# Attention maps of both token tiles in one stage, with a PSUM ring in the planner

## The chip, the core and the metric

One core of a Trainium2 chip runs the whole program. The metric is the device time of one execution in microseconds (us). Names used below: PE is TensorE (matmuls and transposes), DVE is VectorE, ACT is ScalarE, POOL is GpSimd, SP issues the weight transfers. PSUM is the memory that PE writes its results to; a PSUM tile here is one bank of 128 x 512 fp32.

## The reference

Two layers; each has a mixer part, a convolutional feed-forward part and a gated embedding. The change lies in the mixer part:

```python
proj = u @ w_in      # -> qa ka va | qi ki wi | qb kb vb | gate_a gate_b
# mixer A: 8 heads, one shared key/value head, 64 best keys of each query by the indexer
logit = einsum('bthd,btkd->bthk', qa, k_sel) * scale_a
o_a = einsum('bthk,btkd->bthd', softmax(where(valid, logit, -inf)), v_sel)
# mixer B: 4 heads with two softmax maps each, over all earlier keys
a1 = softmax(where(causal, s1, -inf)); a2 = softmax(where(causal, s2, -inf))
o_b = einsum('bhts,bshe->bthe', a1 - lam * a2, vb)
o_b = rms_norm(o_b, g_subln) * (1 - lam_init)
mix = sigmoid(gate_a) * (o_a @ w_branch_a) + sigmoid(gate_b) * (o_b @ w_branch_b)
h = h + mix @ w_out
```

There are 256 tokens and 1024 channels. Mixer A is computed densely: the selection is an additive mask of 0 or -1e30.

## The kernel before, in words

The 256 tokens are two tiles of 128 (`i` = 0 and 1); tile `i` sees 128 * (i + 1) keys. All weights stream from HBM as 128 chunks of 128 x 1024 a layer. Each chunk is split into a high part `wh` (ACT, line 164) and a rest `wl` (DVE, line 179), and each product is three matmuls: high by `wh`, high by `wl`, rest by `wh` (lines 352 to 354, function `gemm_a`). One chunk feeds 12 such matmuls. These streams are the main work of PE: the projections and gates read `u`, the two branch products read `o`, the output product reads `m`. The branch products come in a fixed order: 48 matmuls for mixer B, a point at which the program insists that mixer A is finished, then 48 for mixer A.

The mixers' own work is small and is slipped between these streams by a planner (`class Side`). It holds Python generators ("threads"), each a chain of steps that issue instructions and yield how long the step should keep PE, DVE and ACT busy. After every 12 stream matmuls `tick` runs each thread that the planner's model thinks ready, by priority. The model only decides where in the program an instruction stands; on the chip every engine takes its instructions in that order and waits by semaphores. `side.until(flag)` ticks with no stream between, until a step is done: once for mixer B ("ob") at the end of the gates, and once for mixer A before its branch product.

A map step (`maps`, lines 585 to 608) makes the scores of 4 maps of one token tile and one half of the heads (`hq`). PE first adds the mask (line 596: identity by mask, bf16, on the whole 128-row array), then the products (line 628 for B, 633 for A), which contract over 64 rows and so use half of the array, two at a time. DVE takes maxima (`mx`, `nb`), ACT takes 4 exponentials with sums (line 605). Each map step takes 2 of the 4 PSUM tiles named `tp`. Then the thread normalises on DVE (line 645 or 689), transposes on PE (line 620), copies on ACT (`pt`, line 621), and multiplies by the values on PE (line 656 for B, 699 for A). Mixer B also needs the norm of its result: squares on ACT (`osq`, line 661), `oss` on DVE, a power on POOL (line 262), `ob` on DVE (line 669); `ob` is transposed at the end (line 315, names `ident,ob`). Eight map steps in a layer: 2 mixers x 2 halves of the heads x 2 token tiles.

Of the kernel before, what the change touches and what calls it, by code (L numbers as in the profile page):

```python
# [9 lines left out]
F32 = mybir.dt.float32  # L10
# [7 lines left out]
P = 128  # L18
# [27 lines left out]
ORDER_A = [(0, 1), (1, 1), (0, 0), (1, 0)]  # L46
ORDER_B = [(0, 1), (0, 0), (1, 1), (1, 0)]
# [12 lines left out]

class Side:
# [6 lines left out]
    def __init__(self):  # L68
        self.threads = []
        self.pe = self.dve = self.act = 0.0  # L70

    def spawn(self, gen, prio=1):
        self.threads.append([prio, gen, 0.0])
        self.threads.sort(key=lambda t: t[0])
# [8 lines left out]
    def tick(self):  # L83
        start = self.pe
        for t in list(self.threads):
            if t[2] > self.pe or self.dve > self.pe + LIMIT_US or self.pe > start + SIDE_US:
                continue
            try:
                pe, dve, act = next(t[1])
            except StopIteration:  # L90
                self.threads.remove(t)
                continue
            self.pe += pe
# [16 lines left out]
def decoder_kernel(ctx: ExitStack, tc: tile.TileContext, x, pT, ws, fc, tb, gf, rope, out):  # L110
# [170 lines left out]
    def b4(name, dt=F32):  # L281
        return blk.tile([P, 4, L], dt, tag="blk", name=name)

    class HL:
# [18 lines left out]
    def split_T2(srcs, hf, k0, scale, x, between=None):  # L303


        hi, lo = x.two(4 * hf + k0)
        n = 1 if callable(scale) else 2
        pts = []
        for a in range(0, 2, n):
            pt = ps_tp.tile([P, 2, L], F32, name="tp")[:, :n, :]  # L310
# [16 lines left out]
    def split_T_side(srcs, hf, scale, x, flag):  # L327
        for k0 in (0, 2):
            split_T2(srcs, hf, k0, scale, x)
            yield 0.45, 0.8, 0.3  # L330
        flags.add(flag)
# [86 lines left out]
    def transposed(srcs, nb, dst):  # L418

        for b0 in range(0, nb, 2):  # L420
            n = min(2, nb - b0)
            pt = ps_tp.tile([P, 2, L], F32, name="tp")
# [19 lines left out]
    for l in range(DEPTH):  # L442
# [44 lines left out]
        def index_side(pi):  # L487
# [18 lines left out]
            pt = ps_tp.tile([P, 2, L], F32, name="tp")  # L506
# [9 lines left out]
            for i in range(2):  # L516
                S = P * (i + 1)
                rel = b4("rel")[:, :, :S]
                ps = [ps_tp.tile([P, 2, L], F32, name="tp") for _ in range(2)]
# [42 lines left out]
        def heads_side(pr, nm, is_q):  # L562

            rows, rq = [], []
            for i in range(2):
# [13 lines left out]
                yield 0.0, (2.8 if nm == "kb" else 2.2), 0.0  # L579
            rqs[nm] = rq  # L580
            qT[nm] = b4("qT")
# [4 lines left out]
        def maps(qn, product, i, hq, mk):  # L586
# [3 lines left out]
            mx, nb, sums = (sm.tile([P, 2, 2], F32, name=nm, bufs=4) for nm in ("mx", "nb", "sums"))  # L590
# [6 lines left out]
            for m in range(2):  # L597
                for r in range(2):
                    product(pss[r][:, m, :S], 2 * hq + m, r, slice(i * P, (i + 1) * P), S)
            for r in range(2):  # L600
                nc.vector.reduce_max(mx[:, r, :], pss[r][:, :, :S], axis=AX.X)
            nc.vector.scalar_tensor_tensor(nb, mx, -1.0, rq, op0=ALU.mult, op1=ALU.mult)
            for r in range(2):
                for m in range(2):
                    nc.scalar.activation(pe[:, 2 * m + r, :], pss[r][:, m, :S], AF.Exp,  # L605
                                         bias=nb[:, r, m:m + 1], scale=rq[:, r, m:m + 1],
                                         accum_out=sums[:, r, m:m + 1])
            return pe, sums

        def ptrans(src, nh, i):  # L610
# [4 lines left out]
            for a in range(0, n, 4):  # L615
                w = min(4, n - a)
                pt = ps_tp.tile([P, 4, P], F32, name="tp")
# [17 lines left out]
        def mixer_b(hq, i):  # L635
            while not {"qb", "kb"} <= flags:
                yield NONE
            pe, sums = maps("qb", product_b, i, hq, cmb)
            yield 0.9 + 0.9 * i, 0.8 + 0.6 * i, MA + MB * i
# [12 lines left out]
            po = ps_tp.tile([P, 4, P], F32, name="tp")[:, 0:2, :]  # L652
# [28 lines left out]
        def mixer_a(hq, i):  # L681
            while not {"qa", "mask"} <= flags:
                yield NONE
            pe, sums = maps("qa", product_a, i, hq, mask[i])
            yield 0.9 + 0.9 * i, 0.8 + 0.6 * i, MA + MB * i
# [5 lines left out]
            yield 0.0, 0.9 + 0.3 * i, 0.0  # L691
            pt = ptrans(pe, 4, i)
            yield 0.5 + 0.5 * i, 0.0, 0.5 + 0.5 * i
            nb = i + 1
            ptv = pt[:, :4 * nb, :].rearrange("p (m r s) t -> p m r s t", r=2, s=nb)
            po = ps_tp.tile([P, 2, L], F32, name="tp")[:, 0, :].rearrange("p (m t) -> p m t", t=P)
# [11 lines left out]
        def o_side():  # L708
            while not {("b", hq, i) for hq, i in ORDER_B} <= flags:
                yield NONE  # L710
            for k0 in (0, 2):
                split_T2([ob[:, 0, :], ob[:, 1, :]], 1, k0, gsub, o_parts())
                yield 0.45, 0.8, 0.3
            flags.add("ob")
# [6 lines left out]
        for hq, i in ORDER_B:  # L721
            side.spawn(mixer_b(hq, i), 1)
# [4 lines left out]
        for hq, i in ORDER_A:  # L727
            side.spawn(mixer_a(hq, i), 1)
# [19 lines left out]
        side.until(lambda: {("a", hq, i) for hq, i in ORDER_A} <= flags)  # L748
# [31 lines left out]
        def ffn_T(i, hf):  # L780
            for k in (0, 2):
                pt = ps_tp.tile([P, 4, P], F32, name="tp")[:, 0:2, :]
# [45 lines left out]
        def products(c):  # L828


            if c - C_UP >= 2:
                made[c] = chunk(l, c)
                acc = ps_tp.tile([P, 2, L], F32, name="tp")
                part_products(c, acc, range(KD))
                return acc
            if c == C_UP:
# [3 lines left out]
                accs = [ps_tp.tile([P, 2, L], F32, name="tp") for _ in cs]  # L840
# [226 lines left out]
```

## Time and profile before

| | |
|---|---|
| median of 3 runs | 789.13 us (789.01 to 789.47) |
| profiled execution, its own time | 788.99 us |
| its span, first to last instruction | 787.2 us |
| PE busy / chain that ended last, PE share | 778.2 us (99%) / 91% |
| DVE, ACT, POOL busy | 588.8, 501.3, 162.0 us |
| granted clock of TensorE | 1.00 of full speed |
| map steps of the two layers | near 65 to 126 us and 450 to 511 us |

The page gives busy time, the chain of work that ended last and the costliest groups of instructions. The timeline gives instructions in order of time; neighbours alike are merged, so the time from one row's start to the next row's start is what a step really takes on its engine, and the duration of a single matmul, which overlaps the next, is not.

### The profile page before, as it was taken

Reading aid. Unit: us, or ns where it says so; the run is one execution under the profiler, and the core shown is the slowest. Engines: PE = TensorE matmul, PEld = TensorE weight load, DVE = VectorE, ACT = ScalarE, POOL = GpSimd, SP = SyncE. Lnnn points to the kernel's source line nnn. Section 1 sums busy time; section 2 is a strip of 40 time slices with the busy share of each in tenths; the row PEclk is TensorE's granted clock in tenths of the full one; section 3 lists DMA queues with packets and bytes.
Section 4 is the critical chain, followed back from the end, with each engine's and each line's share of the span. In section 5 each row is a group of like instructions: output and inputs, shape, how many; then the busy total and the mean of one; then the engine's idle time right before and its main releaser. Section 6 shows DMA issues by size and latency. Waiting matters only on the chain.

```text
span 787.2 us, 11678 instructions
## 1 busy us (share of the span) xinstructions
PE 778.2 (99%) x4025; PEld 646.3 (82%) x4025; DVE 588.8 (75%) x1128; ACT 501.3 (64%) x886; POOL 162.0 (21%) x162
## 2 busy tenths in 40 slices
PE   8999999999999999999999999999999999999997
PEld 6877886788888888888888778778888888888886
DVE  5987997675887778854687889768668878795643
ACT  6766757455877777553576486565468777773541
POOL 0240300000344442000123213000104444400000
PEclk9999999999999999999999999999999999999999
DMA  8654353462665656646465344445636656558521
GB/s 325 213 167 155 114 198 124 152 227 94 219 206 183 197 194 210 230 157 228 134 195 177 126 142 165 148 131 193 205 121 207 204 177 204 178 181 289 183 85 54
DMA packets 40188, 139.51 MB, mean 177 GB/s; under 512 B 4544, under 2 KB 5696, under 8 KB 40128
## 3 DMA queue, kind: packets, MB, share of 16 engines
q1 hardware_dynamic: 39264, 136.91, 52.3%
q10 hardware_dynamic: 864, 1.84, 0.7%
q8 instruction: 32, 0.52, 0.3%
q14 instruction: 28, 0.23, 0.1%
HBM read 137.69 MB, written 1.05 MB: 176 GB/s over the span
## 4 chain that ended last, share of the span: by engine, by line
PE 91%; DVE 3%; ACT 3%; POOL 1%; issue 1%; DMA 1%; SPq 0%; DVEq 0%; ACTq 0%
PE tp L824 21%; PE acc L352 12%; PE acc L354 12%; PE acc L353 12%; PE tp L826 11%; PE acc L926 5%; PE acc L925 5%; PE acc L927 5%; ACT pe L605 2%; PE tp L315 2%; DVE wl L179 1%; PE tp L620 1%; PE tp L699 1%; PE tp L656 1%; PE tp L633 1%
## 5 line engine op out<-in xcount | busy, mean ns | idle before, releaser
L164 ACT ACTIVATE wh<-raw 128x1024 fp32r<-128x1024 f32 x254 | 264.1, 1058 | 37.3 <-PE acc L927 18.0
L179 DVE TENSOR_TENSOR wl<-raw,wh 128x1024 fp32r<-128x1024 f32 x178 | 213.7, 1220 | 26.5 <-ACT wh L164 26.3
L824 PE MATMUL tp<-u,wh 128*128 128x512 f32 x704 | 177.1, 392 | 0.0
L824 PEld LDWEIGHTS tp<-u,wh 128*128 128x128 f32 x704 | 126.3, 189 | 22.3
L352 PE MATMUL acc<-wh,u 128*128 128x512 f32 (+1 forms) x336 | 133.7, 398 | 0.0
L353 PE MATMUL acc<-wl,u 128*128 128x512 f32 (+1 forms) x336 | 130.5, 388 | 0.0
L354 PE MATMUL acc<-wh,u 128*128 128x512 f32 (+1 forms) x336 | 130.5, 388 | 0.0
L176 POOL TENSOR_TENSOR wl<-raw,wh 128x512 fp32r<-128x512 f32 x76 | 98.4, 1295 | 142.9 <-ACT wh L164 60.9
L826 PEld LDWEIGHTS tp<-u,wl 128*128 128x128 f32 x704 | 96.6, 190 | 7.2
L826 PE MATMUL tp<-u,wl 128*128 128x256 f32 x704 | 98.8, 282 | 0.0
L858 DVE SCALAR_TENSOR_TENSOR cv<-tp,fc,cv 128x255 f32<-128x255 f32 (+1 forms) x176 | 84.1, 478 | 3.1
L352 PEld LDWEIGHTS acc<-wh,u 128*128 128x128 f32 x336 | 63.1, 188 | 13.2 <-issue 0.7
L354 PEld LDWEIGHTS acc<-wh,u 128*128 128x128 f32 x336 | 63.1, 188 | 12.9
L353 PEld LDWEIGHTS acc<-wl,u 128*128 128x128 f32 x336 | 63.2, 188 | 11.6 <-DVE wl L179 0.2
L853 DVE TENSOR_TENSOR tp<-tp,cl 128x256 f32<-128x256 f32 x88 | 38.0, 432 | 45.9 <-ACT cl L851 45.4
L925 PE MATMUL acc<-wh,g 128*128 128x512 f32 x176 | 68.9, 391 | 0.0
L927 PE MATMUL acc<-wh,g 128*128 128x512 f32 x176 | 68.5, 389 | 0.0
L926 PE MATMUL acc<-wl,g 128*128 128x512 f32 x176 | 68.5, 389 | 0.0
L854 ACT ACTIVATE cv<-tp,fc 128x256 f32<-128x256 f32 x88 | 49.6, 564 | 25.8 <-DVE tp L853 25.3
L276 POOL TENSOR_SCALAR sst<-ss 128x2 f32<-128x2 f32 (+1 forms) x8 | 5.0, 628 | 258.7 <-ACT junk L268 258.5
L175 DVE TENSOR_TENSOR wl<-raw,wh 128x514 fp32r<-128x514 f32 x76 | 53.6, 705 | 0.0
L851 ACT ACTIVATE cl<-tp 128x256 f32<-128x256 f32 x88 | 33.5, 381 | 28.9 <-PE tp L826 28.7
(180 smaller groups left out, 1038.9 us busy)
## 6 DMA issues: line engine op xcount, KB each, us to landing
raw<-ws SPq DMA_DIRECT2D x254, 512.0 KB, 3.5
raw<-ws SPq DMA_DIRECT2D x4, 256.0 KB, 5.0
gb<-gf ACTq DMA_DIRECT2D x2, 512.0 KB, 4.6
out<-h SPq DMA_DIRECT2D x3, 256.0 KB, 2.0
h<-x SPq DMA_DIRECT2D x2, 256.0 KB, 4.3
h<-x SPq DMA_DIRECT2D x1, 512.0 KB, 6.4
px<-pT ACTq DMA_DIRECT2D x2, 256.0 KB, 2.8
tbl<-tb SPq DMA_DIRECT2D x1, 256.0 KB, 7.3
```

What stands on the lines that cost most here:

```text
L164: nc.scalar.activation(wh, raw, AF.Copy)
L176: nc.gpsimd.tensor_tensor(wl[:, b], raw[:, b], wh[:, b].bitcast(F32), op=ALU.subtract)
L179: nc.vector.tensor_sub(wl, raw, wh.bitcast(F32))
L352: nc.tensor.matmul(o, a, wh, start=q == 0, stop=False)
L353: nc.tensor.matmul(o, a, wl, start=False, stop=False)
L354: nc.tensor.matmul(o, b, wh, start=False, stop=q == nk - 1)
L824: nc.tensor.matmul(acc, wh[:, k, :], u.pair(k), start=k == 0, stop=False)
L826: nc.tensor.matmul(acc[:, 0, :], wl[:, k, :], u.hi(k), start=False, stop=k == KD - 1)
L858: nc.vector.scalar_tensor_tensor(c[:, sh:], pu[:, :L - sh], w[:, 2 - sh:3 - sh], c[:, sh:], op0=ALU.mult, op1=ALU.add)
L925: nc.tensor.matmul(acc[i], a, wh, start=k == 0, stop=False)
L926: nc.tensor.matmul(acc[i], a, wl, start=False, stop=False)
L927: nc.tensor.matmul(acc[i], b, wh, start=False, stop=k == NF - 1)
```

## The change

Both token tiles of one half of the heads now form one map step. All four mask products stand first, then all eight half-array products; the step takes all four PSUM tiles at once. The exponentials of both tiles follow, and each tile's remaining work becomes a thread of its own. The hand-written orders of the steps are gone. The planner gets a ring that models when the four PSUM tiles come free: a thread announces with `Room(n)` how many it needs, and isn't run before the model has them free. The planned cost of one step of `kb` rises from 2.8 to 3.4.

```diff
-ORDER_A = [(0, 1), (1, 1), (0, 0), (1, 0)]
-ORDER_B = [(0, 1), (0, 0), (1, 1), (1, 0)]
+EXP_US = (1.75, 2.2)
+BANK_US = 0.9
...
+    def room(self, n):
+        return all(self.free[(self.taken + j) % 4] <= self.pe for j in range(n))
...
+            if not self.room(t[3]):
+                continue
+            taken, t[3] = self.taken, 0
             try:
-                pe, dve, act = next(t[1])
+                got = next(t[1])
+                while isinstance(got, Room):
+                    t[3] = got.n
+                    got = next(t[1]) if self.room(got.n) else NONE
...
+            until = self.pe + BANK_US
+            if exp:
+                self.exp = until = max(self.exp, self.pe + LAG_US + dve) + exp[0]
+            for j in range(taken, self.taken):
+                self.free[j % 4] = until
...
-        def maps(qn, product, i, hq, mk):
+        def scores(qn, product, i, hq, mk):
...
-            pss = [ps_tp.tile([P, 2, L], F32, name="tp") for _ in range(2)]
+            pss = [tp([P, 2, L]) for _ in range(2)]
             mk2 = mk.unsqueeze(1).broadcast_to([P, 2, n])
             for r in range(2):
                 nc.tensor.matmul(pss[r][:, :, S - n:S], identb, mk2, start=True, stop=False, skip_group_check=True)
-            for m in range(2):
+            def products():
+                for m in range(2):
+                    for r in range(2):
+                        product(pss[r][:, m, :S], 2 * hq + m, r, slice(i * P, (i + 1) * P), S)
+            def exps():
...
+            return products, exps
+
+        def maps(ready, qn, product, hq, mk, rest, prio):
+            while not ready():
+                yield NONE
+            yield Room(4)
+            todo = [scores(qn, product, i, hq, mk(i)) for i in (1, 0)]
+            for products, _ in todo:
+                products()
+            got = [exps() for _, exps in todo]
+            yield 2.0, 2.2, 2 * MA + MB, sum(EXP_US)
+            for i, g in zip((1, 0), got):
+                side.spawn(rest(hq, i, *g), prio)
...
-        def mixer_a(hq, i):
-            while not {"qa", "mask"} <= flags:
-                yield NONE
-            pe, sums = maps("qa", product_a, i, hq, mask[i])
-            yield 0.9 + 0.9 * i, 0.8 + 0.6 * i, MA + MB * i
+        def mixer_a(hq, i, pe, sums):
...
+            yield Room(i + 1)
             pt = ptrans(pe, 4, i)
             yield 0.5 + 0.5 * i, 0.0, 0.5 + 0.5 * i
+            yield Room(1)
...
-        for hq, i in ORDER_B:
-            side.spawn(mixer_b(hq, i), 1)
+        for hq in range(2):
+            side.spawn(maps(lambda: {"qb", "kb"} <= flags, "qb", product_b, hq, lambda i: cmb, mixer_b, 1), 1)
...
-        for hq, i in ORDER_A:
-            side.spawn(mixer_a(hq, i), 1)
+        for hq in range(2):
+            side.spawn(maps(lambda: {"qa", "mask"} <= flags, "qa", product_a, hq, lambda i: mask[i], mixer_a, 1), 1)
```

Three places show how the order of instructions moves. The first is PE, first layer, first map steps of mixer B (`cmb` is the causal mask, `qT` the transposed queries and keys). Before:

```order
L596 LDWEIGHTS identb
L596 MATMUL tp<-cmb,identb 128x2x128
L596 LDWEIGHTS identb
L596 MATMUL tp<-cmb,identb 128x2x128
L628 MATMUL tp<-qT 128x256 x4
L596 LDWEIGHTS identb
L596 MATMUL tp<-cmb,identb 128x2x128
L596 LDWEIGHTS identb
L596 MATMUL tp<-cmb,identb 128x2x128
L628 MATMUL tp<-qT 128x128 x4
```

And PE at the same place of the program after the change:

```order
L631 LDWEIGHTS identb
L631 MATMUL tp<-cmb,identb 128x2x128
L631 LDWEIGHTS identb
L631 MATMUL tp<-cmb,identb 128x2x128
L631 LDWEIGHTS identb
L631 MATMUL tp<-cmb,identb 128x2x128
L631 LDWEIGHTS identb
L631 MATMUL tp<-cmb,identb 128x2x128
L681 MATMUL tp<-qT 128x256 x4
L681 MATMUL tp<-qT 128x128 x4
```

The two half-array runs have become one. The second place is PE in the second layer, from the end of the gates into the branch products. Before, the last steps of mixer A stand between stream matmuls of the branch product, 12 apart (`va` are the values, `o` the branch input):

```order
L354 MATMUL acc<-wh,o 128x512
L699 MATMUL tp<-pt,va 64x256 x4
L620 MATMUL tp<-ident,pe 128x128 x4
L352 MATMUL acc<-wh,o 128x512
L353 MATMUL acc<-wl,o 128x512
L354 MATMUL acc<-wh,o 128x512
L352 MATMUL acc<-wh,o 128x512
```

After the change, PE at the end of the second layer's gates (`prv` are mixer B's values, `ob` its result):

```order
L385 MATMUL acc<-wh,u 128x512
L707 MATMUL tp<-prv,pt 128x128 x6
L673 MATMUL tp<-ident,pe 128x128 x24
L748 MATMUL tp<-pt,va 64x256 x6
L345 MATMUL tp<-ident,ob 128x128 x4
L748 MATMUL tp<-pt,va 64x256 x4
L345 MATMUL tp<-ident,ob 128x128 x4
L748 MATMUL tp<-pt,va 64x256 x2
L383 MATMUL acc<-wh,o 128x512
L384 MATMUL acc<-wl,o 128x512
```

Half of mixer B's value products, all transposes of mixer A and all its value products now stand in one run with no stream matmul between. (In the first layer the run is `ident,pe` x12, `pt,va` x6, `ident,pe` x12, `pt,va` x6, between the two branch products.) The third place is ACT at that end of the second layer, after the change, from the exponentials of mixer A's second half on:

```order
L644 ACTIVATE pe,sums<-tp,nb,rq 128x256 x4
L644 ACTIVATE pe,sums<-tp,nb,rq 128x128 x4
L189 ACTIVATE wh<-raw 128x1024 x2
L787 ACTIVATE tg<-acc,rsh 128x512 x2
L189 ACTIVATE wh<-raw 128x1024
L712 ACTIVATE osq,oss<-tp 128x128 x4
L674 ACTIVATE pt<-tp 128x512 x6
L752 ACTIVATE o<-tp 128x2x128 x2
```

The copies `pt` that the value products need stand behind all of these; before, mixer B had been finished earlier, and one or two `pt` copies at a time stood between single `wh` rows.

## Rows read from the trace of the kernel before

**Rows 1.** Page, part 1: busy us (share of the span) and instructions

```profile
PE 778.2 (99%) x4025; PEld 646.3 (82%) x4025; DVE 588.8 (75%) x1128; ACT 501.3 (64%) x886; POOL 162.0 (21%) x162
```

**Rows 2.** Timeline of PE, first map steps: start us, us, engine, line, tiles, count

```profile
64.87 0.39 PE L596 MATMUL tp<-cmb,identb 128*128 128x256 bf16 x2
65.19 1.13 PE L628 MATMUL tp<-qT 64*128 64x256 f32 x8
66.26 0.39 PE L596 MATMUL tp<-cmb,identb 128*128 128x256 bf16 x2
66.58 0.72 PE L628 MATMUL tp<-qT 64*128 64x128 f32 x8
67.22 0.50 PE L352 MATMUL acc<-wh,u 128*128 128x512 f32 x1
```

**Rows 3.** Timeline of PE, second map steps of mixer B and the next stream

```profile
70.12 0.60 PE L596 MATMUL tp<-cmb,identb 128*128 128x256 bf16 x2
...
73.05 0.50 PE L352 MATMUL acc<-wh,u 128*128 128x512 f32 x1
...
84.07 1.14 PE L620 MATMUL tp<-ident,pe 128*128 128x128 f32 x8
```

**Rows 4.** Waits: engine, line, waited for: us in total, times, longest

```profile
PE tp L596 <- ACT pe L605: 0.9, 3, 0.5
```

**Rows 5.** Timeline of PE, first map step of mixer A

```profile
117.48 0.60 PE L596 MATMUL tp<-mk,identb 128*128 128x512 bf16 x2
118.02 1.14 PE L633 MATMUL tp<-kT,qT 64*128 64x256 f32 x8
```

**Rows 6.** Timeline of PE, value products and transposes of mixer A

```profile
132.85 1.08 PE L699 MATMUL tp<-pt,va 128*64 128x256 f32 x8
133.86 1.09 PE L620 MATMUL tp<-ident,pe 128*128 128x128 f32 x8
134.71 0.47 PE L352 MATMUL acc<-wh,o 128*128 128x512 f32 x1
```

**Rows 7.** Timeline of ACT, mixer A of the first layer

```profile
120.77 0.56 ACT L605 ACTIVATE pe<-tp,nb,rq 128x256 f32<-128x256 f32 x1 [5.86 <-PE tp L633]
...
126.06 0.49 ACT L605 ACTIVATE pe<-tp,nb,rq 128x128 f32<-128x128 f32 x1
...
129.54 1.13 ACT L164 ACTIVATE wh<-raw 128x1024 fp32r<-128x1024 f32 x1
130.49 1.34 ACT L737 ACTIVATE tg<-acc,rsh 128x512 f32<-128x512 f32 x2
131.62 1.17 ACT L621 ACTIVATE pt<-tp 128x512 f32<-128x512 f32 x2
```

**Rows 8.** Timeline of DVE, mixer A of the first layer

```profile
122.19 1.22 DVE L179 TENSOR_TENSOR wl<-raw,wh 128x1024 fp32r<-128x1024 f32 x1
...
128.26 0.17 DVE L687 RECIPROCAL rcp<-sums 128x4 f32<-128x4 f32 x1
...
129.52 0.17 DVE L687 RECIPROCAL rcp<-sums 128x4 f32<-128x4 f32 x1
...
130.52 0.17 DVE L687 RECIPROCAL rcp<-sums 128x4 f32<-128x4 f32 x1
```

**Rows 9.** Timeline of ACT, squares of mixer B in the second layer

```profile
488.59 0.27 ACT L661 ACTIVATE osq<-tp 128x128 f32<-128x128 f32 x1
...
489.09 1.07 ACT L164 ACTIVATE wh<-raw 128x1024 fp32r<-128x1024 f32 x1
```

**Rows 10.** Timeline of POOL, the power for mixer B's norm

```profile
489.76 0.19 POOL L261 TENSOR_SCALAR pw<-oss 128x2 f32<-128x2 f32 x1 [5.09 <-DVE oss L664]
490.03 0.69 POOL L262 TENSOR_TENSOR ff<-pw,mhalf 128x2 f32<-128x2 f32 x1
```

**Rows 11.** Windows at the end: length, PE, PEld, DVE, ACT, POOL busy, PEclk, DMA

```profile
782.00:783.00 1.00, 0.82 (x7) 0.61 (x6) 0.89 (x3) 0.15 (x1) 0.00 (x0) 1.00 0.03 10
786.00:787.00 1.00, 0.00 (x0) 0.00 (x0) 0.00 (x0) 0.00 (x0) 0.00 (x0) 0.91 0.00 0
```

More of the change, by code (lines that the diff above doesn't have):

```diff
@@ L69, in __init__ @@
         self.threads = []
-        self.pe = self.dve = self.act = 0.0
+        self.pe = self.dve = self.act = self.exp = 0.0
+        self.free, self.taken = [0.0] * 4, 0
+    def room(self, n):
+        return all(self.free[(self.taken + j) % 4] <= self.pe for j in range(n))
     def spawn(self, gen, prio=1):
-        self.threads.append([prio, gen, 0.0])
+        self.threads.append([prio, gen, 0.0, 0])
         self.threads.sort(key=lambda t: t[0])
@@ L92, in tick @@
                 continue
+            pe, dve, act, *exp = got
+            if got is not NONE:
+                t[3] = 0
             self.pe += pe
             end = self.pe
+            until = self.pe + BANK_US
[3 more added lines that the diff above has]
+                self.free[j % 4] = until
             if dve:
@@ L282, in b4, with tp @@
         return blk.tile([P, 4, L], dt, tag="blk", name=name)
+    def tp(shape):
+        side.free[side.taken % 4] = side.pe + BANK_US
+        side.taken += 1
+        return ps_tp.tile(shape, F32, name="tp")
     class HL:
@@ L328, in split_T_side @@
         for k0 in (0, 2):
+            yield Room(2 if callable(scale) else 1)
             split_T2(srcs, hf, k0, scale, x)
@@ L421, in transposed @@
             n = min(2, nb - b0)
-            pt = ps_tp.tile([P, 2, L], F32, name="tp")
+            pt = tp([P, 2, L])
             for j in range(n):
@@ L505, in index_side @@
                 yield 0.0, 2.8, 0.0
-            pt = ps_tp.tile([P, 2, L], F32, name="tp")
+            yield Room(2)
+            pt = tp([P, 2, L])
             for j in range(2):
@@ L517, in index_side @@
                 S = P * (i + 1)
+                yield Room(2)
                 rel = b4("rel")[:, :, :S]
-                ps = [ps_tp.tile([P, 2, L], F32, name="tp") for _ in range(2)]
+                ps = [tp([P, 2, L]) for _ in range(2)]
                 for b in range(2):
@@ L596, in maps @@
                 nc.tensor.matmul(pss[r][:, :, S - n:S], identb, mk2, start=True, stop=False, skip_group_check=True)
-            for m in range(2):
-                for r in range(2):
[L599 to L608, printed above, removed]
+            def products():
[3 more added lines that the diff above has]
+            def exps():
+                for r in range(2):
+                    nc.vector.reduce_max(mx[:, r, :], pss[r][:, :, :S], axis=AX.X)
+                nc.vector.scalar_tensor_tensor(nb, mx, -1.0, rq, op0=ALU.mult, op1=ALU.mult)
+                for r in range(2):
+                    for m in range(2):
+                        nc.scalar.activation(pe[:, 2 * m + r, :], pss[r][:, m, :S], AF.Exp,
+                                             bias=nb[:, r, m:m + 1], scale=rq[:, r, m:m + 1],
+                                             accum_out=sums[:, r, m:m + 1])
+                return pe, sums
+            return products, exps
[10 more added lines that the diff above has]
+                side.spawn(rest(hq, i, *g), prio)
         def ptrans(src, nh, i):
@@ L633, in product_a, with mixer_b @@
             nc.tensor.matmul(o_, qT["qa"][rs_, b, ts], kT[rs_, :S], start=False, stop=True, skip_group_check=True)
-        def mixer_b(hq, i):
-            while not {"qb", "kb"} <= flags:
-                yield NONE
-            pe, sums = maps("qb", product_b, i, hq, cmb)
-            yield 0.9 + 0.9 * i, 0.8 + 0.6 * i, MA + MB * i
+        def mixer_b(hq, i, pe, sums):
             rcp = sm.tile([P, 2, 2], F32, name="rcp", bufs=4)
@@ L708, in o_side @@
         def o_side():
-            while not {("b", hq, i) for hq, i in ORDER_B} <= flags:
+            while not {("b", hq, i) for hq in range(2) for i in range(2)} <= flags:
                 yield NONE
             for k0 in (0, 2):
+                yield Room(1)
                 split_T2([ob[:, 0, :], ob[:, 1, :]], 1, k0, gsub, o_parts())
@@ L747, in decoder_kernel @@
             gemm_a(o["x"], range(4, 8), stream(l, C_BR + 2 * hf), 512, ev_b)
-        side.until(lambda: {("a", hq, i) for hq, i in ORDER_A} <= flags)
+        side.until(lambda: {("a", hq, i) for hq in range(2) for i in range(2)} <= flags)
         px = sm.tile([P, 2, L], F32, name="px", **T2)
@@ L839, in products @@
                     made[c_] = chunk(l, c_)
-                accs = [ps_tp.tile([P, 2, L], F32, name="tp") for _ in cs]
+                accs = [tp([P, 2, L]) for _ in cs]
                 for ks in (range(KD // 2), range(KD // 2, KD)):
```

24 lines of the change are left out of this document (14 added, 10 removed).

## Prediction

> **What bounds the kernel now.** I read the page first, then PE's timeline around the map steps, then ACT's and DVE's timelines at the same places. The page has PE busy for 99% of the span [rows 1], so time is won only where PE spends time on something else than its matmul columns, and lost wherever PE must stand still. The reader is to see three such places. A half-array run costs more than its columns [rows 2]; the second half of the heads waits for PSUM banks that the exponentials still read [rows 3, 4]; and a stream restarts slowly after each interruption [rows 2, 3]. Everything else on ACT, DVE and POOL is hidden as long as stream matmuls stand between a step and the next one that needs it. That last point is what the change touches most.
>
> **Gain 1: fewer turns between whole and half array.** Eight half-array products on 256 columns take 65.19 to 66.26 = 1.07 us, on 128 columns 66.58 to 67.22 = 0.64 [rows 2]. The difference of 0.43 is the price of 128 columns for all eight, so 1.07 contains 0.86 of columns and 0.21 of fixed cost for entering and leaving the half array. Two mask products of 256 columns take 0.32 (64.87 to 65.19), two of 512 columns 0.54 (117.48 to 118.02) [rows 2, 5]: 0.22 of columns and 0.10 fixed. The pair of steps took 64.87 to 67.22 = 2.35; the merged step has each fixed cost once: 0.10 + 0.44 + 0.21 + 0.86 + 0.43 = 2.04. So 0.31 saved per merged pair, and 4 pairs in each of 2 layers: 2.5 us. The lower bound is 0 (if the fixed cost belongs to each change of length and not to the array), the upper 0.31; I take the upper, since mask and product runs of both lengths give the same fixed part.
>
> **Gain 2: waits for banks.** The second pair of mixer B takes 70.12 to 73.05 = 2.93 against 2.35 for the first, with the same instructions: 0.58 of waiting [rows 2, 3]. The second layer has the same, and mixer A once waits 0.5; PE's own part of it is listed as 0.9 in 3 waits [rows 4]. That is 0.9 to 1.7, and I take 1.7. It goes away because the order now puts 36 or more stream matmuls between the halves of mixer B, 8.1 us at 0.226 each (the 36 more matmuls between 73.05 and 84.07 than between 67.22 and 70.12 took 8.1 us more [rows 2, 3]), and 36 (24 of `o` and 12 of `u` in the first layer) between those of mixer A. All exponentials of a merged step are over about 7.5 us after its start (below), so the banks are free. Without that cover the wait would come back, at about 0.6 each.
>
> **Gain 3: fewer restarts.** Twelve stream matmuls between two map steps take 67.22 to 70.12 = 2.90, where 12 x 0.226 is 2.71: 0.19 for one restart after the half array [rows 2, 3]. Counted in the order of instructions from the first map step to the point where the branch products run without a break, the runs of stream matmuls go from 28 to 17 in both layers together. Most of those that go stood behind transposes, whose restart I did not price and take as less; with 0.12 as a middle the 11 are worth 1.3 us, between 0.5 and 2.1.
>
> The gains sum to 2.5 + 1.7 + 1.3 = 5.5 us.
>
> **Loss: two runs with nothing between.** At the end of mixer A in the first layer, and of both mixers in the second, the program insists that the mixers be finished, and the steps now stand in one run on PE (the second place of the order). I add up each engine's queue there, from the start of mixer A's second map step as time 0. Prices, start to start: an exponential of 256 columns 0.54, of 128 columns 0.435 (120.77 to 126.06 holds eight of the first kind and one `wh`; 126.06 to 129.54 eight of the second); `wh` 0.95; `tg` 0.57; a `pt` copy 0.5, with 0.62 until its data is there [rows 7]; `wl` 1.15; normalising four maps of 256 columns 1.26, of 128 columns 1.0 [rows 8]; a square 0.25 [rows 9]; the power on POOL 1.0 with its first step [rows 10]; 8 transposes 0.85, 8 value products 1.0 [rows 6].
>
> First layer. PE: the map step 2.3 (512-column masks), 24 stream matmuls 5.6, then 12 transposes, done at 9.3. ACT: from a step's start to the first exponential it took 117.48 to 120.77 = 3.3 [rows 5, 7]; with two more masks ahead 3.5. Eight exponentials end at 7.4, and the order then has three `wh` (10.25) before the copies: two copies are there at 11.4. So PE stands from 9.3 to 11.4, then does value products until 12.9. DVE, whose order has two `wl` and two evictions of the branch product in between (the first `wl` waits for its `wh`, 8.4), normalises the second half only at 14.3: the next 12 transposes end at 14.6, copies at 15.2, and the last value products at 16.5. PE's own work is 8.0 + 5.6 = 13.6. Loss 2.9 us. What could hide it is the branch product of mixer B, but that now stands ahead of the run.
>
> Second layer. PE: 2.3 + 5.7 = 8.0, value products of mixer B until 9.3, 8 transposes until 10.1; the next 4 need a PSUM bank that a `pt` copy frees. ACT: 7.4, two `wh` 9.3, two `tg` 10.45, one `wh` 11.4, four squares 12.4, first copy 13.0. PE goes on in small pieces (13.1 to 14.0), then needs the banks that mixer B's result still holds. They are freed by `ob`: DVE has to normalise first (13.0, again behind two `wl`), then `oss` 13.4, POOL 14.4 and 15.4, `ob` 15.0 and 16.0 (0.6 for two short operations, an estimate from rows 8). From 16.1 PE has 3.9 us of value products and transposes left: 20.0. PE's own work would have ended at 8.0 + 7.7 = 15.7. Loss 4.3 us.
>
> The bounds: each loss is at least the one copy that must follow the last transpose before any value product, about 1.1 us; upwards a late transfer in front of a `wh` could add about 1 us to each chain, so 1.1 to 4 and 1.1 to 5.5. I take the sums, 2.9 and 4.3, since in the rows the same kinds of instructions follow each other on ACT without a gap.
>
> After the runs nothing is late: four to five chunks are split ahead, and the streams that follow stand in the same order as before. What becomes late elsewhere: mixer B's transposes in the first layer need a normalisation that DVE ends just then; I put nothing on it. The planner's ring and `kb`'s cost have no instructions of their own; they act through the order, which is counted above.
>
> **Sum.** -5.5 + 2.9 + 4.3 = +1.7 us on the profiled execution's 788.99 (span 787.2 and 1.8 around it): 790.7. The median of the runs lies 0.14 above the profiled one: 790.8 us.
>
> **Rivals.**
> *The gains prevail.* If ACT and DVE are less far behind than I add up, each run costs only the copy that cannot be hidden, 2 x 1.1, and the time is 789.1 - 5.5 + 2.2 = 785.8. For it: DVE is busy 75% and ACT 64% of the time [rows 1], so a queue that is behind catches up fast. Against it: at these places the order itself puts two or three `wh` and the gates' `tg` ahead of the copies, and that is not a matter of averages. Chance 0.2.
> *The clock falls in the second layer's run.* In the trace PE's last work ends at 782.82, and the granted clock is still full for at least 3 us and falls between 786 and 787 [rows 11]. After the change PE would stand from 10.1 to 13.1 and then do only transposes until 16.1. If that is long enough, the 3.9 us after it take twice as long, and the next stream starts at 1.2 instead of 2.4 GHz, some 2 us more until it rises (an estimate: half of a stretch as long as those 3.9 us): about 5 to 6 us, 796. It decides from the point where the pause outlasts what the last rows allow. Chance 0.1.
> The Trainium skill (TensorE: Matmul & The Clock Gate, "HAM oscillation — how this bites in real kernels") holds that a long pause of PE sends the clock back to half, and its section "Part 4: PE-mode transpose" says that these do not count as activity in the same way. By that rule this rival would be the likelier one, since the stretch with only transposes is the longer; no row of the kernel before has such a stretch.
> *The banks bind at once.* A merged step takes all four banks, so one late reader anywhere stops it, where a step of two banks could pass. If each of the four second halves waits as it did, 0.6 each, 2.4 come back: 793.2. For it: that is what happened with two banks [rows 3, 4]. Against it: 8 us of stream now stand between. Chance 0.1.
> *The forecast*, chance 0.6, with a range of its own of 789.0 to 793.0.
>
> **How the numbers follow.** A measurement can tell about 0.2%, 1.58 us, so faster means under 787.5 and slower above 790.7. The forecast lies at that upper edge: of its 0.6 some 0.32 are slower, 0.27 the same and 0.01 faster. The first rival gives 0.16 faster and 0.04 same, the two others 0.2 slower. Together 0.17, 0.31 and 0.52. The range reaches from just above the first rival's time to just beyond the banks', and leaves out the clock and the far half of the first rival: 786.2 to 794.0.
>
> **What would show it.** Right: map steps of 2.0 to 2.3 us on PE with no wait inside; PE idle for 2 to 3 us behind the 12 transposes of the first layer, and about 4 us in the run at the end of the second layer's gates, with ACT `pt` and DVE `ob` as releasers; the two exponential groups followed by `wh` and `tg` before `pt`. Wrong: if PE has no waits in these runs, the loss is mis-sized; if a merged step still shows 0.3 us of extra per tile, gain 1 is; if PEclk shows less than 1.00 near the second run, the clock decided.

## The result, and the profile after

The changed kernel takes 795.23 us (median of 5 runs, 794.99 to 797.15); the kernel before, on the same chip, 789.17 (789.01 to 789.47). The ratio is 1.0073, 95% interval [1.0062, 1.0085]: slower, on the side that I gave 0.52, but 4.4 us beyond the forecast and outside the range of 786.2 to 794.0. The profiled execution has a span of 794.0 us against 787.2 and a mean granted clock of 0.996 (0.992 to 0.996 in the five executions) against 1.000. PE is busy as long as before within 0.3 us [rows 1], so the 6.8 us appear as time in which it stood; inside the busy time, what the change saved hides what slower matmuls cost (below):

```profile
PE 777.9 (98%) x4025; PEld 650.4 (82%) x4025; DVE 589.3 (74%) x1128; ACT 501.7 (63%) x886; POOL 165.2 (21%) x162
```

PE's timeline at the first merged map step (start us, us, engine, line, tiles, count) answers to [rows 2]:

```profile
65.13 0.61 PE L631 MATMUL tp<-cmb,identb 128*128 128x256 bf16 x4
65.67 1.58 PE L681 MATMUL tp<-qT 64*128 64x256 f32 x16
67.18 0.50 PE L383 MATMUL acc<-wh,u 128*128 128x512 f32 x1
```

From 65.13 to 67.18 is 2.05 us, where I had worked out 2.04; mixer A's takes 2.26. No merged step shows a wait inside.

The run at the end of the second layer's gates, PE's timeline; a bracket gives the idle time before a row and what ended it:

```profile
514.47 1.50 PE L707 MATMUL tp<-prv,pt 128*128 128x128 f32 x12
515.80 1.04 PE L673 MATMUL tp<-ident,pe 128*128 128x128 f32 x8
519.76 1.14 PE L673 MATMUL tp<-ident,pe 128*128 128x128 f32 x8 [2.92 <-ACT pt L674]
521.89 1.97 PE L673 MATMUL tp<-ident,pe 128*128 128x128 f32 x8 [0.99 <-DVE ob L720]
523.79 2.83 PE L748 MATMUL tp<-pt,va 128*64 128x256 f32 x12
526.55 1.12 PE L345 MATMUL tp<-ident,ob 128*128 128x128 f32 x4
...
529.88 0.50 PE L383 MATMUL acc<-wh,o 128*128 128x512 f32 x1
```

The map step ahead of it starts at 506.63. So PE goes on at +13.1 with the second transposes, as I had added up (13.1), and both `ob` end near +15.2 and +16.3 (15.0 and 16.0). From there the forecast had 3.9 us of work, and it took 7.0. Windows of the same stretch (length, busy us of PE, PEld, DVE, ACT, POOL, then PEclk and DMA) show why:

```profile
518.00:520.00 2.00, 0.24 (x2) 0.24 (x3) 1.93 (x12) 2.00 (x11) 0.00 (x0) 1.00 0.91 283
520.00:521.00 1.00, 0.90 (x8) 0.59 (x6) 0.28 (x3) 0.74 (x3) 0.70 (x2) 1.00 0.77 311
521.00:522.00 1.00, 0.11 (x1) 0.11 (x2) 0.58 (x2) 0.54 (x2) 0.83 (x3) 0.51 0.28 102
...
524.00:526.00 2.00, 2.00 (x12) 1.04 (x10) 0.00 (x0) 0.68 (x2) 0.00 (x0) 0.50 0.00 0
526.00:528.00 2.00, 2.00 (x12) 1.04 (x10) 0.85 (x2) 0.88 (x3) 0.00 (x0) 0.54 0.00 0
528.00:530.00 2.00, 2.00 (x17) 0.99 (x14) 1.18 (x2) 1.38 (x4) 0.00 (x0) 1.00 0.00 0
```

The sixth number of a row, after the five engines, is PEclk: 1.00 until 521, then 0.50, the lower of the two levels (1.2 instead of 2.4 GHz), until just before 528. The engine had stood from 516.8 to 519.8, done eight transposes, and stood again. The twelve value products from 523.79 take 2.76 us to the next row; the same twelve take 1.45 in the first layer (eight took 1.0 in [rows 6]), in the run that answers to the first loss (PE's timeline):

```profile
138.80 1.47 PE L673 MATMUL tp<-ident,pe 128*128 128x128 f32 x12
142.84 1.52 PE L748 MATMUL tp<-pt,va 128*64 128x256 f32 x12 [2.57 <-ACT pt L674]
144.29 1.09 PE L673 MATMUL tp<-ident,pe 128*128 128x128 f32 x8
...
146.21 1.52 PE L748 MATMUL tp<-pt,va 128*64 128x256 f32 x12
147.66 0.50 PE L383 MATMUL acc<-wh,o 128*128 128x512 f32 x1
```

Here the map step starts at 130.96, and the run ends at +16.7 (forecast 16.5). In this execution the clock stayed at 1.00 through that run.

ACT's timeline ahead of the 2.92 us, second layer, shows what stands in front of the copies that PE waits for; in [rows 7] two copies followed a single `wh` and the `tg`:

```profile
514.06 2.02 ACT L189 ACTIVATE wh<-raw 128x1024 fp32r<-128x1024 f32 x2
515.96 1.28 ACT L787 ACTIVATE tg<-acc,rsh 128x512 f32<-128x512 f32 x2
517.10 1.08 ACT L189 ACTIVATE wh<-raw 128x1024 fp32r<-128x1024 f32 x1
...
519.05 1.15 ACT L674 ACTIVATE pt<-tp 128x512 f32<-128x512 f32 x2
```

One place I had put at nothing. Mixer B's transposes in the first layer, PE, and what DVE does meanwhile:

```profile
92.24 0.82 PE L673 MATMUL tp<-ident,pe 128*128 128x128 f32 x6
93.44 0.74 PE L673 MATMUL tp<-ident,pe 128*128 128x128 f32 x4 [0.38 <-DVE pe L694]
94.57 0.50 PE L673 MATMUL tp<-ident,pe 128*128 128x128 f32 x2 [0.38 <-DVE pe L694]
94.82 0.48 PE L383 MATMUL acc<-wh,u 128*128 128x512 f32 x1
```

```profile
90.22 1.22 DVE L204 TENSOR_TENSOR wl<-raw,wh 128x1024 fp32r<-128x1024 f32 x1
...
91.82 0.62 DVE L694 SCALAR_TENSOR_TENSOR pe<-pe,cf 128x128 f32<-128x128 f32 x2
...
92.81 0.88 DVE L694 SCALAR_TENSOR_TENSOR pe<-pe,cf 128x256 f32<-128x256 f32 x2
```

Twelve transposes take 2.58 us (92.24 to 94.82) instead of some 1.3: the tiles are normalised while PE is already there, and one `wl` stands between the first and the second. The second layer has the same for six transposes, 1.63 us.

Added up from PE's timeline, stretch by stretch, against the kernel before: map steps -4.3, streams -2.1, the rest of the side work +4.4 in the first layer (run 3.1, mixer B's transposes 1.3) and +8.6 in the second (run about 7.5, of it 3.1 more than I had added up behind `ob`; mixer B's transposes 1.0), start +0.3: 6.9 of the 6.8 us.

### The profile page after: what moved, and what is told of

Same layout as the page of the kernel before. It is cut to its first block, busy times and chain, and to the rows that moved or that the text cites. A ratio compares the mean times of both kernels' runs of the same rounds, so it can differ in the third digit from the quotient of the medians.

```text
span 794.0 us, 11685 instructions
## 1 busy us (share of the span) xinstructions
PE 777.9 (98%) x4025; PEld 650.4 (82%) x4025; DVE 589.3 (74%) x1128; ACT 501.7 (63%) x886; POOL 165.2 (21%) x162
## 3 DMA queue, kind: packets, MB, share of 16 engines
q10 hardware_dynamic: 864, 1.84, 0.8%
## 4 chain that ended last, share of the span: by engine, by line
PE 85%; DVE 8%; ACT 4%; issue 1%; DMA 1%; POOL 0%; SPq 0%; ACTq 0%; POOLq 0%
PE tp L874 20%; PE acc L383 11%; PE tp L876 11%; PE acc L385 11%; PE acc L384 11%; PE acc L975 5%; PE acc L977 5%; PE acc L976 5%; ACT pe L644 2%; DVE wl L204 2%; PE tp L345 2%; DVE mx L640 1%; ACT wh L189 1%; PE tp L748 1%; DMA h<-x 1%
## 5 line engine op out<-in xcount | busy, mean ns | idle before, releaser
L644 ACT ACTIVATE pe<-tp,nb,rq 128x256 f32<-128x256 f32 (+1 forms) x64 | 31.7, 515 | 34.7 <-DVE nb L641 34.7
```

## The experiments

**1. Is it the clock?** The changed kernel with matmuls of no use in the second layer's pauses:

```diff
+                if l == 1 and n == 4 * nb and side.tail:
+                    for _ in range(KEEP.get(side.blk, 0)):     # KEEP = {2: 11, 4: 4}
+                        nc.tensor.matmul(keep[0], identb, cmk, start=True, stop=True)
+                    side.blk += 1
                 pt = tp([P, 4, P])
```

> The changed kernel plus 15 idle-work matmuls on PE (mask identity by a zero tile of 512 columns in bf16, about 0.23 to 0.27 us each, result unused) in the run at the end of the second layer: 11 before the transposes that waited 2.92 us for a pt copy, 4 before those that waited 0.99 us for ob. Nothing else moves. Theory 'clock': the last part of that run was slow (7.0 us where I had added up 3.9) because the granted clock stood at half from 521.0 to 527.8; with PE kept at work it stays at 1.00, the twelve value products take 1.45 us again in place of 2.76, and the time is 795.2 - 3.1 = 792.1 us. Rival 'chain': the last part is bound by copies on ACT and ob on DVE, and the clock only fell because PE stood; then the time stays at 795.2 (within 0.5) even with the clock at 1.00.

Measured: 1.0048 [1.0030, 1.0067] of before. PE's timeline in that run:

```profile
517.81 2.54 PE L677 MATMUL acc<-cmk,identb 128*128 128x512 bf16 x11
...
523.02 1.09 PE L682 MATMUL tp<-ident,pe 128*128 128x128 f32 x8
524.07 1.51 PE L757 MATMUL tp<-pt,va 128*64 128x256 f32 x12
525.52 0.66 PE L350 MATMUL tp<-ident,ob 128*128 128x128 f32 x4
...
528.28 0.50 PE L388 MATMUL acc<-wh,o 128*128 128x512 f32 x1
```

The last transposes and all value products now take 523.02 to 528.28 = 5.3 us; the same instructions took 521.89 to 529.88 = 8.0, and in both kernels they begin 15.3 us after the start of the map step ahead. The clock is 1.00 in every window from 518 to 532, and the twelve products take 1.45. So the clock cost 2.7 us, and the chain of copies does not hold this part. The total shows less of it (the intervals of this and of the changed kernel touch), because in the profiled execution the clock fell in the first layer's run, which got no such matmuls; the one execution with a mean clock of 0.999 took 792.61 us. The window in the first layer's run:

```profile
142.00:144.00 2.00, 1.37 (x8) 0.81 (x10) 1.97 (x6) 1.06 (x3) 0.00 (x0) 0.54 0.78 260
```

**2. and 5. Does PE wait for copies behind splits?** Experiment 2 was to hold the splits back, but the flag was set one stage late: the three `wh` still stood ahead of `pt`, and the wait of 2.90 us stayed.

```diff
-        if nx["cur"] >= 2:
+        if nx["cur"] >= 2 and not nx["off"]:
...
+            if hq and qn == "qa":
+                nx["off"] = True
             for i, g in zip((1, 0), got):
```

> The changed kernel, but between mixer A's second map step and the end of the mixers no chunk is split (no wh on ACT, no wl on DVE); the splits are caught up behind. PE's order is unchanged. Theory 'queue': PE waited in both runs for pt copies that stood behind three wh of 0.95 us. In the first layer the wait of 2.57 us nearly goes (to 0 to 0.5), in the second that of 2.92 falls to about 0 to 1 and ob comes 2 to 3 us earlier: together -4.5 to -5.5. If the half clock came from that pause, it goes as well, -3.1: about 787.0 us; if the clock still falls, about 790. Rival 'late splits': the weights withheld are missing right behind the runs, the stream waits for wh and wl, and the time stays near 795.

Measured: 1.0119 [1.0101, 1.0137], slower still; it says nothing on the queue, but it shows the rival's price. Behind the run PE and then ACT wait:

```profile
541.88 0.50 PE L384 MATMUL acc<-wl,o 128*128 128x512 f32 x1 [1.69 <-DVE wl L204]
```

```profile
545.24 1.06 ACT L189 ACTIVATE wh<-raw 128x1024 fp32r<-128x1024 f32 x1 [9.62 <-DMA raw<-ws]
```

A split that is withheld keeps its `raw` buffer, so the next transfers start late: SP waits up to 23.0 us for a `wl` here, 14.5 in the changed kernel. Experiment 5 sets the flag with the map step itself and gives everything back as soon as mixer A is finished (the planner's model is charged at the old place, so the order on PE does not move):

```diff
+    def put(do):
+        if nx["skip"]:
+            later.append(do)
+        else:
+            flush()
+            do()
...
             got = [exps() for _, exps in todo]
+            if hq and qn == "qa":
+                nx["skip"] = True
...
+        def mixed():
+            if {("a", hq, i) for hq in range(2) for i in range(2)} <= flags:
+                nx["skip"] = False
+                flush()
```

> As e2, with the edit where it belongs: from mixer A's second map step on, no wh and no wl is issued until the mixers are finished, then all that were withheld at once; the planner's model and PE's order are unchanged. ACT now has pt directly behind the exponentials (and tg, osq). Theory 'queue': the wait of 2.57 us in the first layer goes to 0.3 or less, that of 2.92 in the second to about 0.5, ob comes 2.5 us earlier, and the clock stays full in both runs: 795.2 - 2.3 - 2.5 - 2.8 = 787.6 us, if the stream behind finds its weights. Rival 'late splits': withheld wl keep the raw buffers, so the transfers start late and the stream waits some us for them behind the run: the runs are short, and the time is still 792 or more. Rival 'PSUM': the pauses stay, because a bank and not the copy is late: 795.

Measured: 787.79 us, 0.9975 [0.9964, 0.9987] of before: the first theory, within 0.2 us. ACT's first copies in the first layer, and PE's waits in both runs:

```profile
139.41 1.57 ACT L696 ACTIVATE pt<-tp 128x512 f32<-128x512 f32 x3 [0.48 <-PE tp L695]
```

```profile
140.55 1.51 PE L775 MATMUL tp<-pt,va 128*64 128x256 f32 x12 [0.30 <-ACT pt L696]
...
514.84 0.66 PE L695 MATMUL tp<-ident,pe 128*128 128x128 f32 x4 [0.46 <-ACT pt L696]
516.03 1.71 PE L695 MATMUL tp<-ident,pe 128*128 128x128 f32 x12 [0.54 <-DVE ob L742]
```

The pauses of 2.57 and 2.92 are now 0.30 and 0.46, nothing of PE's order has changed, and PEclk is 1.00 in every window of both runs. ACT's first copies now wait for PE (0.48 us), and what PE still waits for are the copies behind its own last transposes and once an `ob` (0.54).

**3. and 8. The stall in mixer B's transposes.** Experiment 3 moves only the split between mixer B's normalisations one stage later, with the `put` of experiment 5:

```diff
+            nx["skip"] = True
             yield 0.0, 0.7 + 0.3 * i, 0.0
```

> The changed kernel, but the split that stands on DVE (and ACT) between the normalisations of mixer B's first and second token tile comes one stage of the stream later. PE's order is unchanged. Theory 'DVE queue': the stalls inside mixer B's transposes (2.58 us for twelve in the first layer, 1.63 for six in the second, where PE needs about 1.3 and 0.65) come from the one wl of 1.15 us that stands between; without it they go, -1.2 and -0.9: 793.1 us. Rival: the normalisations wait for something else (sums of the exponentials), and the time stays at 795.2 (within 0.5).

Measured: 1.0053 [1.0038, 1.0068]. The twelve transposes take 93.50 to 94.92 = 1.42 us, the six of the second layer 0.57 instead of 1.63, so the stall was that one split. The total is less clear, since the intervals of this and of the changed kernel touch. In the profiled execution two things hide the gain: the first map step begins 1.3 us later (66.39 against 65.13), ahead of anything the edit moves, and the clock falls in the first layer's run as well.

```profile
93.50 1.67 PE L695 MATMUL tp<-ident,pe 128*128 128x128 f32 x12
94.92 0.48 PE L405 MATMUL acc<-wh,u 128*128 128x512 f32 x1
```

Experiment 8 is 3 and 5 together:

```diff
-        if nx["skip"]:
+        if nx["skip"] or nx["off"]:
             later.append(do)
```

> e5 and e3 together: withheld splits behind mixer A's second map step, and the one split between mixer B's normalisations moved one stage later; PE's order as after the change. Theory: the stalls inside mixer B's transposes, still there in e5 (0.37 + 0.38 and 0.68 us of waiting for DVE, some 1.2 and 0.9 in all), go as well and nothing else moves: 787.8 - 1.6 = 786.2 us (e3 alone gained about 1.6 by its ratio, 1.0053 against 1.0073). Rival: both edits take splits away from the same stretch of the stream, chunks come late, and the time is 787.8 or more.

Measured: 785.51 us (785.33 to 785.61), 0.9936 [0.9922, 0.9949] of before, and 785.45, 0.9950 [0.9938, 0.9963], when it was run again: the lowest time here, and it beats both kernels. (The interval of this second run overlaps that of experiment 4, so which of these two is faster is less sure.) Of PE's waits in the mixers these are left (waited for: us in total, times, longest):

```profile
PE tp L779 <- ACT pt L699: 0.6, 2, 0.3
PE tp L698 <- DVE ob L746: 0.5, 1, 0.5
PE tp L698 <- ACT pt L699: 0.5, 1, 0.5
```

**10. What a merged step is worth.** Experiment 8 with each tile's products directly behind its own masks:

```diff
-            todo = [scores(qn, product, i, hq, mk(i)) for i in (1, 0)]
-            for products, _ in todo:
-                products()
+            todo = []
+            for i in (1, 0):
+                todo.append(scores(qn, product, i, hq, mk(i)))
+                todo[-1][0]()
```

> e8 with one thing undone: in each map step the two masks of a token tile are followed at once by that tile's eight half-array products (mask, products, mask, products), as before the change; banks, places in the program and all other engines as in e8. Theory: each of the eight steps has the fixed cost of the mask run and of the half array twice again, 0.31 us, and the time is 2.5 us above e8's: ratio to e8 1.003, 788.0 us. Rival: the fixed costs belong to changes of length, or the time PE gains is only waited for elsewhere: within 0.5 us of e8.

> The kernel of e8 once more, beside e10 on the same chip: 785.5 us, within 0.5, with the clock at full in every execution; every theory has the same here, and only the difference to e10 is asked for.

Measured on one chip: 787.97 us, 0.9983 [0.9974, 0.9992], against 785.45. The step takes 2.36 us again:

```profile
65.41 0.39 PE L654 MATMUL tp<-cmb,identb 128*128 128x256 bf16 x2
...
67.77 0.50 PE L406 MATMUL acc<-wh,u 128*128 128x512 f32 x1
```

2.36 - 2.05 = 0.31 a step (2.05 in the changed kernel and in experiment 8), and all eight steps show it: mixer A's take 2.57 against 2.26. That is 2.5 us, and 2.5 is what the medians differ by; the lowest executions differ by 1.9 (787.27 and 785.33), so the total is good to about half a us. Gain 1 is shown.

**4. The ring alone.** Map steps of one tile, in the orders written by hand, with the ring and `kb`'s cost of the change:

```diff
-            yield Room(4)
-            todo = [scores(qn, product, i, hq, mk(i)) for i in (1, 0)]
+            yield Room(2)
+            products, exps = scores(qn, product, i, hq, mk(i))
```

> The planner's ring and kb's cost as after the change, but the map steps of one token tile each, two banks at a time, in the order written by hand before. Theory: the loss of the change lies in the merged step, which shifts work to the end and makes the two runs; the ring alone keeps 12 or more stream matmuls between transposes and value products, so no long wait, some of the waits for banks go (up to 1.7 us), and the time is 787.5 to 789.5 us. Rival: the ring itself, which holds threads back, makes the runs; then this kernel is near 793 to 795 us without any merged step.

Measured: 787.12 us, 0.9964 [0.9953, 0.9975] of before. The planner's new model is a gain by itself, without any merged step, and PE's timeline has no run at either end. Experiment 7 has merged steps without the ring and no run either; so what made the runs is the ring, with its numbers, together with a step that takes all four banks.

**7. The merged step alone.** Ring off, `kb` as before:

```diff
     def room(self, n):
-        return all(self.free[(self.taken + j) % 4] <= self.pe for j in range(n))
+        return True
```

> The merged map steps with the planner's ring switched off (every thread is told that there is room) and kb's cost as before. Mixer B's two merged steps now stand back to back, mixer A's with 12 matmuls between; the run at the end of the second layer is gone. Theory 'banks': a second step that follows at once waits for the exponentials of the first, about 4 us a layer for mixer B (the last of eight exponentials ends 7.5 us after a step's start, and the step itself takes 2.1) and 1 to 2 for mixer A, so 789.2 - 4.2 + 8 + 3 = 796 us. Rival: PE's products only wait for the bank they write, the exponentials free one bank after the other, and the loss is 0.6 a step: 787 to 788 us.

Measured: 811.03 us, 1.0269 [1.0251, 1.0287]. Mixer B's second step stands directly behind the first and gets its banks one by one, where [rows 4] had waits of 0.5 at most:

```profile
70.98 0.27 PE L631 MATMUL tp<-cmb,identb 128*128 128x256 bf16 x1 [2.44 <-ACT pe L644]
72.08 0.35 PE L631 MATMUL tp<-cmb,identb 128*128 128x256 bf16 x1 [0.82 <-ACT pe L644]
72.95 0.37 PE L631 MATMUL tp<-cmb,identb 128*128 128x256 bf16 x1 [0.53 <-ACT pe L644]
...
74.14 2.93 PE L681 MATMUL tp<-qT 64*128 64x256 f32 x16
```

The mechanism is the expected one (4.3 us of waiting here), the size is not: 22 us slower, not 7. Mixer A's steps, for which 1 to 2 us were expected, wait nearly as long: 4.1 us in the first layer, 3.1 of it for DVE's reading of the banks that `ob`'s transposes took. The clock adds to it: PEclk is 0.50 from 74 to 76, and the products behind the waits take 2.86 us instead of 1.51.

**6. and 9. Two other orders.** Experiment 6 has merged steps and no run at either end, by other numbers in the planner (`EXP_US` (0.9, 1.2), `LIMIT_US` 5, `EARLY` 1, `GAP` 10) and these lines:

```diff
+        return not self.pend & set(nxt) and all(self.free[j] <= self.pe + EARLY for j in nxt)
...
-            while not ready():
+            while not ready() or side.pe < side.gap:
...
+            side.gap = side.pe + GAP
```

> The changed kernel with the merged map steps, but other numbers in the planner (its ring lets a thread go 1 us early, counts exponentials as 2.1 us in place of 3.95, allows DVE 5 us of lead, and lets 10 us pass between two map steps) and one rule that a bank holding mixer B's result is not asked for before ob stands in the program. The order that comes out has stream matmuls between all steps: 24 or more behind each map step, 12 between transposes and their value products, no run at either end. Theory: the merged steps are worth what I counted (-4.2) and the waits for banks go (-1.7), and all of the loss came from the runs: 783 to 785 us. Rival 'the merge costs': four banks at once make waits somewhere in any order (inside the steps, or at the transposes behind them), and the time is 787 to 790, no better than the ring alone (787.1).

Measured: 796.52 us, 1.0079 [1.0058, 1.0100]. The theory missed by 12 us; the rival's waits are there, at a higher price than its 787 to 790. PE's timeline at mixer A's second step, and the window behind it:

```profile
123.66 0.27 PE L636 MATMUL tp<-mk,identb 128*128 128x256 bf16 x1 [1.84 <-DVE o L354]
```

```profile
124.00:126.00 2.00, 2.00 (x13) 1.69 (x15) 0.20 (x1) 0.00 (x0) 0.00 (x0) 0.52 0.55 213
```

The fourth mask needs the bank that `ob`'s transposes took shortly before; DVE reads it late. One pause of 1.84 us is followed by half clock; the second layer has pauses of 1.83 and 3.17 with the same effect (PEclk 0.50 from 514 to 516 and from 528 to 530). Experiment 9 merges mixer B's steps alone (its steps for mixer A are those of experiment 4):

```diff
-        for hq in range(2):
-            side.spawn(maps(lambda: {"qa", "mask"} <= flags, "qa", product_a, hq, lambda i: mask[i], mixer_a, 1), 1)
+        for hq, i in [(0, 1), (1, 1), (0, 0), (1, 0)]:
+            side.spawn(maps1(lambda: {"qa", "mask"} <= flags, "qa", product_a, hq, i, lambda i: mask[i], mixer_a, 1), 1)
```

> Merged map steps for mixer B alone; mixer A's are of one token tile, as before the change. The planner's ring stays, with other numbers (exponentials counted as 5.0 us, a bank 0.5, 5 us between two merged steps, DVE 1.6 for a merged step, kb 2.8) and the rule of e6 on banks that hold mixer B's result. Twelve or more stream matmuls stand between all steps, no run at either end. Theory: a merged step is worth 0.3 us where no pause follows from it, so the ring alone (787.1 median, 786.9 where the clock is full) less 4 x 0.3: 785.7 us. Rival: four banks held by one step make waits for the steps behind it in any order, as in e6, and each pause of 2 us brings half clock as well: 789 or more.

Measured: 793.67 us, 1.0035 [1.0023, 1.0048]: the rival's side. Its largest wait is again mixer B's transposes, placed directly behind those of `qr`, with half clock after it:

```profile
96.37 0.74 PE L690 MATMUL tp<-ident,pe 128*128 128x128 f32 x4 [2.03 <-DVE pe L711]
```

```profile
98.00:100.00 2.00, 2.00 (x6) 1.61 (x5) 2.00 (x8) 0.69 (x1) 0.00 (x0) 0.50 0.19 29
```

That wait is for a normalisation, not a bank, so this run doesn't price the four banks. The twelve stream matmuls behind it take 4.43 us instead of 2.85, and at the same place of the second layer PE waits 1.16 us for ACT's copy of `qT`, without a fall of the clock: 4.8 us in all. By its ratio this run lies some 6 us above the 785.7 expected; the rest I did not follow up.

## Why the prediction was right and wrong, by its steps

Two steps failed: the work at the end of the second run was counted at full clock (2.7 us), and mixer B's transposes were put at nothing (2.3 us). They make 5.0 of the 5.1 us between forecast and profiled execution.

- **Gain 1** (-2.5): right, and shown by experiment 10 (2.36 against 2.05 a step, 2.5 us in all).
- **Gain 2** (-1.7): right as far as the trace goes. No merged step waits, and the map steps together are 4.3 shorter where gains 1 and 2 made 4.2. Experiment 4, where the ring alone spaces the steps, bears it out: its unmerged map steps together take 20.0 us where those of the kernel before take 21.5, PE's waits for exponentials are down to 0.2 us from 0.9 [rows 4], and it is 0.36% faster.
- **Gain 3** (-1.3): the streams are 2.1 us shorter, so it was 0.8 too small; no run separates the restarts.
- **First run** (+2.9): 3.1. PE stood 2.57 us where 2.1 were added up, but the end hangs on DVE's normalising of the second half, and the last value products begin at +15.25, forecast 15.2. Experiment 5 confirms the cause: without the splits ahead of the copies the pause is 0.30 us.
- **Second run** (+4.3): the chain was right to 0.3 us up to `ob`. The step that failed is the sentence "From 16.1 PE has 3.9 us of value products and transposes left". It counted them at full clock, and the trace has them at 0.50 until just before 528: 7.0 us. Experiment 1 gives back 2.7 of these 3.1; the other 0.4 is work that was counted too short.
- **The clock rival** (0.1) is what came true. Its place and its cause were as written (a pause, only transposes, the value products at half). The sign that I had named for it, PEclk under 1.00 near the second run, is there. Its price was too high (5 to 6 us, measured 2.7): the clock was full again before the next stream, so the 2 us behind the run did not occur. That its 796 lies near the measured 795.2 is luck, since 2.3 us of that are mixer B's transposes. Its chance was too low, because I judged it by [rows 11], where the clock is full for 3 us after PE's last work. That was one place only: pauses of 1.84 and 2.03 us were followed by half clock in experiments 6 and 9. The sentences from the Trainium skill (TensorE: Matmul & The Clock Gate, "HAM oscillation — how this bites in real kernels") said that by that page this rival would be the likelier one; the trace agrees, PEclk 0.50 from 521 to 528. That no row showed such a stretch was a reason for a wide chance, not for a low one.
- **"I put nothing on it"**: mixer B's transposes cost 1.3 in the first layer and 1.0 in the second (which I had not named at all). DVE does not "end just then": one `wl` of 1.15 us stands between the normalisations, and the four of them follow each other while PE waits. Experiment 3 shows it: without that split the twelve take 1.42 us.
- **Banks bind at once** (0.1) and **the gains prevail** (0.2): neither occurred in the changed kernel. Experiments 6 and 7 show that the first does as soon as the order puts another user of the banks close by.

Forecast +1.7, measured +6.8 on the profiled execution: clock +2.7, the work behind `ob` +0.4, mixer B's transposes +2.3, streams -0.8, start +0.3, the rest within 0.2 of its term.

## What to carry to other kernels

Where steps on a saturated engine are packed together, list for every consumer in the pack what stands ahead of its producer in the *other* engines' queues: splits that nobody needed yet cost PE two pauses and a stall, and issuing them later turned a loss of 0.7% into a gain of 0.5 to 0.6%. Price a pause of PE both ways, with the work behind it at full and at half clock. And test a planner's order by the order it prints: the same merged step gave 785 to 811 us.

## What the runs showed of the hardware that I had not expected

The clock does not answer to a pause in the same way each time. It stayed at 1.00 through the mixers of experiment 8, whose longest pause is 0.54 us, and behind a pause of 1.16 us in experiment 9. After 1.84 (experiment 6), 2.03 (experiment 9) and 2.92 us with eight transposes and a second wait (the changed kernel) it was at 0.50. The first layer's pause of 2.57 left it at 1.00 in the changed kernel's profile, while one of 2.55 at the same place was followed by half clock in experiments 1, 2 and 3 (PEclk 0.54, 0.51 and 0.50 in the window of 2 us with the lowest). In experiment 5 PE did nothing but transposes from 513.34 to 517.67, 4.3 us with pauses of 0.46 and 0.54 in them, and the clock stayed at 1.00. What decides between these stays open.

The Trainium skill (TensorE: Matmul & The Clock Gate, "Part 4: PE-mode transpose") says that transposes do not count as activity as matmuls do. These rows neither show that nor rule it out; they show that a stretch of transposes as long as this one need not cost the clock.

Withholding a split is not free either: in experiment 2 ACT waited 9.62 us for one transfer, since the buffers it would have gone to were still held by chunks not yet split.
